# Token-major gates and branch projections, and regrouped up-projection matmuls, in a one-core decoder block

## The chip, the cores and the metric

The kernel runs on one core of a Trainium2 chip. A core has a matrix engine (TensorE, PE in the profile, with its weight loads listed apart as PEld), a vector engine (VectorE, DVE), a scalar engine (ScalarE, ACT), GpSimd (POOL) and a sync engine (SyncE, SP) that here issues the weight loads. They run side by side and meet by semaphores. On-chip memory is SBUF; TensorE writes its sums to PSUM, from which VectorE and ScalarE read. The metric is the device time of one execution in microseconds (us), the median of several runs.

## The reference, cut to what matters

One layer of a decoder trunk on 256 tokens of width 2048, all in float32. What is computed:

```python
mod = silu(c) @ w_ada + b_ada                      # 2048 x 12288, one row
h = rms_norm(x, g_pre_mix) * (1 + sc1) + sh1
p = h @ w_in + b_in                                # 2048 x 9216
u, v, q, k, v_att, z_pool, gates = split(p)        # six of 512 columns, gates 3 * 2048
y_sgu, y_moba, y_pool = ...                        # three branches, 512 wide each
g = sigmoid(gates)                                 # one per branch and channel
merged = g_sgu*(y_sgu@w_sgu_out) + g_moba*(y_moba@w_moba_out) + g_pool*(y_pool@w_pool_out)
x = x + gt1 * rms_norm(merged @ w_out, g_post_mix)
h = rms_norm(x, g_pre_ffn) * (1 + sc2) + sh2
z = conv3(h @ w_up) + b_conv                       # 2048 x 11264, causal, width 3 over tokens
gate, val = split(z)
x = x + gt2 * rms_norm((gelu(gate) * val) @ w_down, g_post_ffn)
```

## The kernel before

Every large product is made from three matmuls of rounded operands: an operand is split into a high part (fp32r) and a low part (what the rounding left), and high times high, high times low and low times high are added up in PSUM. Activations are split once. Each weight item, 4 chunks of 128 rows by 512 columns (1 MB), is loaded into one of 4 `raw` buffers, copied to `wh` by ScalarE and subtracted to `wl` by VectorE (`prep`, lines 291 to 320), so an item costs two ScalarE and two VectorE instructions of 128x1024. Six `wh` and six `wl` buffers hold three items.

Three routines do the matmuls of an item, all with 12,288 moving columns. `mm_b` (line 223) has weights stationary and the 256 tokens moving: channels come out on partitions, in 48 matmuls of 256 columns. `mm_a` (line 261) has 128 tokens stationary and 512 weight columns moving: tokens come out on partitions, in 24 matmuls of 512 columns. `mm_pairs` (line 241) has weights stationary and moves the high and the low activations, which lie side by side, as one 512-column matmul, followed by a 256-column one with the low weights: 16 such pairs. Its two sums lie in the two halves of a PSUM bank, and `join` (line 254) adds them, by a ScalarE copy and a VectorE add.

The twelve gate blocks (3 branches b by 4 column blocks j, named g00 to g23) are made in two ways. The six with j of 0 or 1 are in the input projection, which runs over k in four splits of 2, 4, 6 and 4 chunks, with `mm_b`, and the partial sums are added in SBUF (`block_use`, line 526). The six with j of 2 or 3 come later, whole, with `mm_pairs` (`gate_use`, line 504), as do the twelve branch projections (`branch_item`, line 783), whose joined result is multiplied by the gate and added up over b; after the third branch the sum is split into `mh` and `ml` for the output projection. Both need channels on partitions, as the output projection takes `mh` and `ml` as its stationary operand, and the bias of a gate is then one number for each partition, added by ScalarE with the sigmoid. PSUM has three buffers of two banks (`ps_acc`); an item of `mm_pairs` takes two of them, one of `mm_a` or `mm_b` takes one.

The order of work is a list of items: input projection, gates with j = 2, branches with j = 0, 1, 2, gates with j = 3, branches with j = 3, output projection, up and down projections of the feed-forward part. Between them are mixed the items of the conditioning product (`w_ada`), which VectorE accumulates (line 390). Each item's loads are issued 4 items ahead, its split is made up to 3 ahead; what follows its matmuls (`pending`) is issued ahead of the next item's matmuls, and the work on `side` one portion after each item. A scheduler then fixes the order on each engine; loads keep their order on SP's queue. The up projection (`up_item`, line 909) runs 88 items of `mm_pairs`: 24 for the first three column blocks in two halves of k, with the second half of `h2x` made between them (line 1112), and 64 in eight blocks with `mm_a` items of the down projection (tile `ps_dn`) in between.

Of the kernel before, what the change touches and what calls it, by code (L numbers as in the profile page):

```python
# [15 lines left out]
P = 128  # L16
# [10 lines left out]
P4_BUFS = 25  # L27
RAW_BUFS = 4
HL_BUFS = 6
JOIN_BUFS = 2  # L30
LOAD_AHEAD = 4
SPLIT_AHEAD = 3
SPLITS = (2, 4, 6, 4)
# [14 lines left out]
def kernel(  # L48
# [16 lines left out]
    joins = ctx.enter_context(tc.tile_pool(name="joins", bufs=JOIN_BUFS))  # L65
# [187 lines left out]

    def join(ps, dst=None):

        m = joins.tile([P, 2, 256], F32, name="join", tag="join") if dst is None else dst
# [244 lines left out]

    cur = {}

    def gate_use(name, kt0):

        def use(w):
            if kt0 == 0:
                cur[name] = [pair_ps("ps_" + name) for _ in range(2)]
            pss = cur[name]
            last = kt0 + 4 == KT  # L510
            mm_pairs(pss, w, hx_of(kt0), kt0 == 0, last)
            if not last:
                return

            def evac():
                g = gate[name] = p4(name)
                b, j = int(name[1]), int(name[2])
                for pr in range(2):
                    join(pss[pr], g[:, pr * 2:pr * 2 + 2])
                bias4(g, g, AF.Sigmoid, 24 + b * 16 + j * 4)  # L520
                if name == "g23":
                    load_sqrt(g[:, 3, 0:1])
            pending.append(evac)
        return use

    def block_use(name, kt0, nk, lo, hi):

        def use(hl_):
            if kt0 == lo:
                cur[name] = acc_ps("ps_" + name)  # L530
            ps = cur[name]
            last = kt0 + nk == hi
            (mm_a if name in "va" else mm_b)(ps, hl_, h_of(kt0), kt0 == lo, last)
            if not last:
                return

            def evac():
                final = hi == KT
                if lo == 0:
# [27 lines left out]
    def presplit_sigmoids(names):  # L567
        def f():
            for name in names:
                b, j = int(name[1]), int(name[2])  # L570
                bias4(gate[name], gate[name], AF.Sigmoid, 24 + b * 16 + j * 4)
        return f


# [207 lines left out]

    def branch_item(b, j):
        def use(w):
            pss = [pair_ps("ps_br") for _ in range(2)]
            mm_pairs(pss, w, lambda i: both(yx[b][i // 2], i % 2), True, True)

            def evac():
                g = gate[gate_name(b, j)]
                for pr in range(2):  # L790
                    gp = g[:, pr * 2:pr * 2 + 2]
                    nc.vector.tensor_tensor(gp, gp, join(pss[pr]), op=ALU.mult)
                if b:
                    g0 = gate[gate_name(0, j)]
                    nc.vector.tensor_tensor(g0, g0, g, op=ALU.add)
                    del gate[gate_name(b, j)]
                if b == 2:
                    mh[j], ml[j] = p4(f"mh{j}", dt=F32R), p4(f"ml{j}", dt=F32R)
                    split_act(mh[j], ml[j], g0)
                    del gate[gate_name(0, j)]  # L800
            pending.append(evac)
        w_item(w_branch[b], 0, 4, j * 512, use, pairs=True)


    ss2 = cp.tile([P, 2, 4], F32, name="ss2")
# [269 lines left out]

    def gate_full(j):
        for b in range(3):
            name = gate_name(b, j)
            for kt0 in range(0, KT, 4):
                w_item(w_in, kt0, 4, block_cols(name), gate_use(name, kt0), pairs=True)  # L1080

    def phase_mix():
        for j in rest[:-1]:
# [140 lines left out]
```

## Time and profile before

| | |
|---|---|
| time, median of 3 runs | 1438.35 us (1433.37 to 1439.8) |
| the profiled execution's own time | 1436.83 us |
| its span, first to last instruction | 1435.1 us |
| TensorE busy, weight loads | 1383.7 us, 1200.9 us |
| VectorE busy | 1120.9 us |
| ScalarE busy | 724.2 us |
| mean granted TensorE clock | 0.993 of full speed |

A busy TensorE is not one at its peak: matmuls are pipelined and the profile's duration of one (400 ns for 512 columns) is longer than the step from one to the next. Steps are read from a window: its length, divided by the matmuls in it.

### The profile page before, as it was taken

What the parts mean: (1) busy time and instruction counts of PE and PEld (TensorE: products, weight loads), DVE (VectorE), ACT (ScalarE), POOL (GpSimd) and SP (SyncE); (2) the same over time, 40 slices, a digit from 0 to 9 for tenths busy, and PEclk for the clock granted to TensorE, in tenths of its full rate; (3) what the DMA queues carried; (4) which work ended last, traced back from release to release, by engine and by line L of the source; (5) the groups of instructions that cost most, each with busy time, mean ns of one, the idle gap of its engine ahead of it and who ended that gap; (6) DMA issues with size and microseconds to landing.
All of it is one profiled execution on the core that took longest, in us unless ns stands there. A gap on an engine that the chain in (4) does not pass through costs nothing.

```text
span 1435.1 us, 20349 instructions
## 1 busy us (share of the span) xinstructions
PE 1383.7 (96%) x8095; PEld 1200.9 (84%) x8095; DVE 1120.9 (78%) x1463; ACT 724.2 (50%) x957; POOL 3.7 (0%) x12
## 2 busy tenths in 40 slices
PE   4998999999999999998999999999999999999997
PEld 3797999999888788886887888888888888888886
DVE  1289877689779988887988987879696867667676
ACT  4543534576855455345345654544444454545453
POOL 0000000000000000000000000000000000000000
PEclk9999999999999999999999999999999999999999
DMA  9799978855777798987985576676766765555551
GB/s 319 289 324 306 319 255 296 279 173 201 281 269 247 244 323 296 336 325 256 346 295 202 206 261 237 210 260 208 254 235 219 256 207 191 190 181 195 182 176 59
DMA packets 183022, 355.52 MB, mean 248 GB/s; under 512 B 5960, under 2 KB 20872, under 8 KB 182928
## 3 DMA queue, kind: packets, MB, share of 16 engines
q1 hardware_dynamic: 182076, 353.07, 71.0%
q8 instruction: 63, 1.03, 0.3%
q10 hardware_dynamic: 852, 1.16, 0.2%
q14 instruction: 31, 0.25, 0.0%
HBM read 352.11 MB, written 2.10 MB: 247 GB/s over the span
## 4 chain that ended last, share of the span: by engine, by line
PE 87%; DVE 7%; DMA 3%; ACT 1%; issue 1%; SPq 0%; DVEq 0%; ACTq 0%
PE ps_up L249 23%; PE ps_up L251 12%; PE ps_g L249 6%; PE ps_dn L273 6%; PE ps_dn L271 6%; PE ps_dn L272 6%; PE ps_g L251 3%; PE ps_g L234 3%; PE ps_g L232 3%; PE ps_g L233 3%; PE ps_out L273 2%; PE ps_out L272 2%; PE ps_out L271 2%; DMA raw<-in_w_in_dram 2%; DVE wl L302 2%; PE ps_br L249 1%
## 5 line engine op out<-in xcount | busy, mean ns | idle before, releaser
L249 PE MATMUL ps_up<-h2x,wh 128*128 128x512 f32 x1408 | 499.3, 400 | 5.3 <-DVE h2x L875 2.8
L301 ACT ACTIVATE wh<-raw 128x1024 fp32r<-128x1024 f32 x248 | 260.9, 1059 | 293.2 <-PE ps_up L249 135.6
L251 PE MATMUL ps_up<-h2x,wl 128*128 128x256 f32 x1408 | 395.9, 282 | 0.0
L302 DVE TENSOR_TENSOR wl<-raw,wh 128x1024 fp32r<-128x1024 f32 x248 | 301.3, 1222 | 106.9 <-ACT wh L301 105.6
L314 ACT ACTIVATE wh<-raw 128x1024 fp32r<-128x1024 f32 x228 | 227.5, 1012 | 253.8 <-PE ps_up L249 76.7
L315 DVE TENSOR_TENSOR wl<-raw,wh 128x1024 fp32r<-128x1024 f32 x228 | 261.7, 1167 | 96.7 <-ACT wh L314 96.1
L249 PEld LDWEIGHTS ps_up<-h2x,wh 128*128 128x128 f32 x1408 | 265.2, 189 | 71.0 <-issue 3.8
L251 PEld LDWEIGHTS ps_up<-h2x,wl 128*128 128x128 f32 x1408 | 267.3, 190 | 1.1 <-issue 0.5
L271 PE MATMUL ps_dn<-wh,ah 128*128 128x512 f32 x352 | 138.1, 392 | 0.0
L273 PE MATMUL ps_dn<-wh,al 128*128 128x512 f32 x352 | 137.2, 390 | 0.0
L272 PE MATMUL ps_dn<-wl,ah 128*128 128x512 f32 x352 | 137.2, 390 | 0.0
L249 PE MATMUL ps_g<-hx,wh 128*128 128x512 f32 x384 | 136.2, 399 | 0.0
L390 DVE SCALAR_TENSOR_TENSOR accb<-raw,cond,accb 128x512 f32<-128x512 f32 (+1 forms) x147 | 106.1, 722 | 10.7 <-DMA raw<-in_w_ada_dram 10.6
L390 DVE SCALAR_TENSOR_TENSOR acca<-raw,cond,acca 128x512 f32<-128x512 f32 (+1 forms) x155 | 112.2, 724 | 0.9 <-DMA acca<-in_b_ada_dram 0.8
L234 PE MATMUL ps_g<-hx,wl 128*128 128x256 f32 x384 | 109.2, 285 | 3.8 <-DVE wl L315 3.8
L232 PE MATMUL ps_g<-hx,wh 128*128 128x256 f32 x384 | 110.0, 286 | 2.3 <-ACT wh L314 2.3
L233 PE MATMUL ps_g<-hx,wh 128*128 128x256 f32 x384 | 108.8, 283 | 0.0
L251 PE MATMUL ps_g<-hx,wl 128*128 128x256 f32 x384 | 107.6, 281 | 0.0
L249 PEld LDWEIGHTS ps_g<-hx,wh 128*128 128x128 f32 x384 | 72.0, 188 | 17.3 <-issue 0.4
L271 PEld LDWEIGHTS ps_dn<-wh,ah 128*128 128x128 f32 x352 | 66.1, 188 | 14.2 <-issue 0.5
L272 PEld LDWEIGHTS ps_dn<-wl,ah 128*128 128x128 f32 x352 | 66.1, 188 | 13.9 <-issue 0.5
L234 PEld LDWEIGHTS ps_g<-hx,wl 128*128 128x128 f32 x384 | 73.7, 192 | 4.9 <-DVE wl L315 4.9
(246 smaller groups left out, 2015.4 us busy)
## 6 DMA issues: line engine op xcount, KB each, us to landing
raw<-in_w_up_dram SPq DMA_DIRECT2D x88, 1024.0 KB, 5.0
raw<-in_w_ada_dram SPq DMA_DIRECT2D x84, 1024.0 KB, 5.2
raw<-in_w_in_dram SPq DMA_DIRECT2D x54, 1024.0 KB, 6.1
raw<-in_w_down_dram SPq DMA_DIRECT2D x44, 1024.0 KB, 5.3
raw<-in_w_in_dram SPq DMA_DIRECT2D x24, 768.0 KB, 5.9
raw<-in_w_out_dram SPq DMA_DIRECT2D x16, 1024.0 KB, 7.0
raw<-in_w_ada_dram SPq DMA_DIRECT2D x16, 768.0 KB, 5.6
x<-in_x_dram SPq DMA_DIRECT2D x8, 512.0 KB, 7.2
```

What stands on the lines that cost most here:

```text
L232: nc.tensor.matmul(ps[:, nb], wh[:, s], xh, start=st, stop=False, skip_group_check=True)
L234: nc.tensor.matmul(ps[:, nb], wl[:, s], xh, start=False, stop=sp, skip_group_check=True)
L249: nc.tensor.matmul(ps[:, nb], wh[:, i, s], xhl, start=first and i == 0, stop=False, skip_group_check=True)
L251: nc.tensor.matmul(ps[:, nb, 256:512], wl[:, i, s], xh, start=False, stop=last and i == n - 1, skip_group_check=True)
L271: nc.tensor.matmul(psv[:, tt], xh[:, s], wh, start=st, stop=False)
L272: nc.tensor.matmul(psv[:, tt], xh[:, s], wl, start=False, stop=False)
L273: nc.tensor.matmul(psv[:, tt], xl[:, s], wh, start=False, stop=sp)
L301: nc.scalar.activation(h[:, :nk], it["raw"][:, :, cs], AF.Copy)
L302: nc.vector.tensor_tensor(l[:, :nk], it["raw"][:, :, cs], h[:, :nk].bitcast(F32), op=ALU.subtract)
L314: nc.scalar.activation(h[:, :n], it["raw"][:, k:k + n, cs], AF.Copy)
L315: nc.vector.tensor_tensor(l[:, :n], it["raw"][:, k:k + n, cs], h[:, :n].bitcast(F32), op=ALU.subtract)
L390: nc.vector.scalar_tensor_tensor(a, raw[:, kk], sc, a, op0=ALU.mult, op1=ALU.add)
```

## The change

The gates and the branch projections now go through `mm_a`, so their results have tokens on partitions. A gate's bias then runs along the row: it is loaded for all partitions from `b_in` (`gate_bias`, a 128x512 tile, 256 KB, on SP's queue), and VectorE adds it; ScalarE makes the sigmoid in one instruction. The branch result is multiplied by the gate straight from PSUM, without a join. After the third branch of a j the sum is transposed to channels on partitions by eight TensorE transposes (`merged_rows`, issued as side work), and split from PSUM. `mm_pairs`, now used by the up projection alone, issues the eight 512-column matmuls of a half item first, then its eight 256-column ones.

```diff
-                xh, xhl = act(i)
                 for nb in range(2):
-                    s = slice(nb * 128, nb * 128 + 128)
-                    nc.tensor.matmul(ps[:, nb], wh[:, i, s], xhl, start=first and i == 0, stop=False,
-                                     skip_group_check=True)
-                    nc.tensor.matmul(ps[:, nb, 256:512], wl[:, i, s], xh, start=False,
-                                     stop=last and i == n - 1, skip_group_check=True)
...
+                    nc.tensor.matmul(ps[:, nb], wh[:, i, nb * 128:nb * 128 + 128], act(i)[1],
+                                     start=first and i == 0, stop=False, skip_group_check=True)
+            for i in range(n):
+                for nb in range(2):
+                    nc.tensor.matmul(ps[:, nb, 256:512], wl[:, i, nb * 128:nb * 128 + 128], act(i)[0],
+                                     start=False, stop=last and i == n - 1, skip_group_check=True)
...
+    def gate_bias(name):
+
+        t = auxs.tile([P, 512], F32, name="gb", tag="aux")
+        ldma(t, bcast(b_in, block_cols(name), 512))
+        return t
...
-            (mm_a if name in "va" else mm_b)(ps, hl_, h_of(kt0), kt0 == lo, last)
+            if name[0] == "g" and last and hi == KT:
+                gb = gate_bias(name)[:, None, :].to_broadcast([P, 2, 512])
+            (mm_a if name[0] in "vag" else mm_b)(ps, hl_, h_of(kt0), kt0 == lo, last)
...
+                if (lo, hi) == (0, KT):
+                    g = gate[name] = p4(name)
+                    nc.vector.tensor_tensor(v2(g), v2(ps), gb, op=ALU.add)
+                    nc.scalar.activation(g, g, AF.Sigmoid)
...
-                    gate[name] = part[name]
+                    g = gate[name] = part[name]
+                    nc.vector.tensor_tensor(v2(g), v2(g), gb, op=ALU.add)
...
-                bias4(gate[name], gate[name], AF.Sigmoid, 24 + b * 16 + j * 4)
+                nc.scalar.activation(gate[name], gate[name], AF.Sigmoid)
...
-                for pr in range(2):
-                    gp = g[:, pr * 2:pr * 2 + 2]
-                    nc.vector.tensor_tensor(gp, gp, join(pss[pr]), op=ALU.mult)
+                nc.vector.tensor_tensor(g, g, ps, op=ALU.mult)
...
+                    side.append([lambda: merged_rows(j)])
...
+        for a in range(4):
+            for tt in range(2):
+                nc.tensor.transpose(pt[:, a, tt * 128:tt * 128 + 128], g[:, tt, a * 128:a * 128 + 128], ident)
+        mh[j], ml[j] = p4(f"mh{j}", dt=F32R), p4(f"ml{j}", dt=F32R)
+        split_act(mh[j], ml[j], pt)
```

`gate_use` is gone: `gate_full` calls `block_items` for whole gates. The two join buffers become two `aux` buffers, shared by the up projection's joins and the bias tiles.

TensorE in the up projection, before: `wh` and `wl` are the split weights, `h2x6` and `h2x7` the activations of two chunks of 128 rows each (high and low), `ps_up` the two PSUM buffers of an item.

```order
L249 MATMUL ps_up_8204<-h2x7_7049,wh_8247 128x512
L251 MATMUL ps_up_8204<-h2x7_7049,wl_8248 128x256
...
L249 MATMUL ps_up_8205<-h2x6_7048,wh_8251 128x512
L251 MATMUL ps_up_8205<-h2x6_7048,wl_8252 128x256
...
L249 MATMUL ps_up_8205<-h2x7_7049,wh_8251 128x512
```

The same place after:

```order
L247 MATMUL ps_up_6210<-h2x7_6095,wh_6156 128x512 x4
L251 MATMUL ps_up_6210<-h2x6_6094,wl_6157 128x256 x4
L251 MATMUL ps_up_6210<-h2x7_6095,wl_6157 128x256 x4
L247 MATMUL ps_up_6211<-h2x6_6094,wh_6160 128x512 x4
L247 MATMUL ps_up_6211<-h2x7_6095,wh_6160 128x512 x4
L251 MATMUL ps_up_6211<-h2x6_6094,wl_6161 128x256 x4
```

The two widths no longer alternate; the number of matmuls of each is what it was.

VectorE at the first branch projections, before: `ps_br` is the product in PSUM, `join` its joined halves, `part_g00` and `part_g10` gates, `acca` and `accb` the sums of the conditioning product.

```order
L258 TENSOR_TENSOR join_4313<-join_4313,ps_br_4269 128x512
L336 TENSOR_TENSOR sh2_128<-fin_4321,bada_116 128x4
L792 TENSOR_TENSOR part_g00_570<-part_g00_570,join_4313 128x512
L258 TENSOR_TENSOR join_4317<-join_4317,ps_br_4270 128x512
L302 TENSOR_TENSOR wl_4334<-raw_4303,wh_4333 128x1024
L792 TENSOR_TENSOR part_g00_570<-part_g00_570,join_4317 128x512
L302 TENSOR_TENSOR wl_4389<-raw_4371,wh_4388 128x1024
```

The same place after:

```order
L783 TENSOR_TENSOR part_g00_558<-part_g00_558,ps_br_3582 128x1024
L336 TENSOR_TENSOR sh2_128<-fin_3618,bada_116 128x4
L315 TENSOR_TENSOR wl_3631<-raw_3607,wh_3630 128x1024
L390 SCALAR_TENSOR_TENSOR acca_3573<-raw_3624,cond_109,acca_3573 128x512
L390 SCALAR_TENSOR_TENSOR accb_3574<-raw_3624,cond_109,accb_3574 128x512
L390 SCALAR_TENSOR_TENSOR acca_3573<-raw_3624,cond_109,acca_3573 128x512
L315 TENSOR_TENSOR wl_3670<-raw_3659,wh_3669 128x1024
L783 TENSOR_TENSOR part_g10_604<-part_g10_604,ps_br_3634 128x1024
L315 TENSOR_TENSOR wl_3674<-raw_3659,wh_3673 128x1024
L786 TENSOR_TENSOR part_g00_558<-part_g00_558,part_g10_604 128x1024
```

Two joins and two multiplications of 128x512 for each branch item became one multiplication of 128x1024.

SP's queue ahead of the last gates of the input projection, before: `raw` are the weight buffers.

```order
L288 DMA raw_3197<-in_w_in_dram 128x4x512
L288 DMA raw_3277<-in_w_in_dram 128x4x512
L288 DMA raw_3363<-in_w_ada_dram 128x4x512
L288 DMA raw_3433<-in_w_in_dram 128x4x512
L288 DMA raw_3517<-in_w_in_dram 128x4x512
L288 DMA raw_3575<-in_w_ada_dram 128x4x512
```

The same place after: `gb` is a bias tile, of which there are two buffers.

```order
L82 DMA gb_2672<-in_b_in_dram 128x512
L288 DMA raw_2722<-in_w_in_dram 128x4x512
L288 DMA raw_2781<-in_w_in_dram 128x4x512
L82 DMA gb_2735<-in_b_in_dram 128x512
L288 DMA raw_2846<-in_w_ada_dram 128x4x512
L82 DMA gb_2794<-in_b_in_dram 128x512
L288 DMA raw_2895<-in_w_in_dram 128x4x512
```

The weight loads behind a `gb` now stand behind its wait for a buffer.

## Rows read from the trace of the kernel before

**Rows 1.** Page, part 1: engine, busy us, share of the span, instructions.

```profile
PE 1383.7 (96%) x8095; PEld 1200.9 (84%) x8095; DVE 1120.9 (78%) x1463; ACT 724.2 (50%) x957; POOL 3.7 (0%) x12
```

**Rows 2.** Page, part 4: the chain that ended last, by engine.

```profile
PE 87%; DVE 7%; DMA 3%; ACT 1%; issue 1%; SPq 0%; DVEq 0%; ACTq 0%
```

**Rows 3.** Windows: us, busy PE, PEld, DVE, ACT, POOL (instructions), granted clock, DMA.

```profile
60.00:150.00 90.00, 82.36 (x624) 75.89 (x623) 76.50 (x112) 40.96 (x47) 0.00 (x0) 1.00 0.95 322
150.00:300.00 150.00, 150.00 (x1146) 145.24 (x1146) 116.89 (x139) 75.25 (x95) 2.84 (x5) 1.00 0.81 275
421.12:482.63 61.51, 55.96 (x306) 48.31 (x305) 60.25 (x82) 31.86 (x42) 0.00 (x0) 0.94 0.69 233
430.00:490.00 60.00, 54.45 (x294) 46.86 (x293) 60.00 (x81) 29.30 (x36) 0.00 (x0) 0.94 0.70 242
```

**Rows 4.** Waits from 421 to 483 us: waiter, releaser, us, times, longest.

```profile
PEld ps_br L249 <- DVE join L258: 6.6, 4, 3.1
ACT join L257 <- DVE part_g L792: 6.5, 3, 4.9
PE ps_br L249 <- DVE join L258: 5.6, 3, 2.7
```

**Rows 5.** TensorE in order of time: start, us, line, tiles, idle before.

```profile
455.20 0.80 PE L249 MATMUL ps_br<-yx,wh 128*128 128x512 f32 x1 [2.40 <-DVE join L258]
```

**Rows 6.** TensorE in a window, tile ps_g by mm_b: 256 columns each.

```profile
216.76:255.63 38.87, 38.87 (x324) 1.00 0.86 300
```

**Rows 7.** The same, tile ps_dn by mm_a: 512 columns each.

```profile
1113.34:1135.15 21.81, 21.81 (x96) 1.00 0.69 234
```

**Rows 8.** The same, tile ps_up by mm_pairs: 512 and 256 columns in turn.

```profile
1135.16:1180.36 45.20, 45.20 (x256) 1.00 0.68 235
1000.68:1045.45 44.77, 44.77 (x256) 1.00 0.69 236
672.13:689.00 16.87, 16.87 (x96) 1.00 0.73 249
```

**Rows 9.** The same, tile ps_g by mm_pairs, gates with j = 2 and 3.

```profile
398.41:421.11 22.70, 22.70 (x128) 1.00 0.84 293
506.05:539.41 33.36, 33.36 (x192) 1.00 0.91 324
```

**Rows 10.** The same, tile ps_br by mm_pairs, branches with j = 3.

```profile
551.38:568.07 16.69, 16.69 (x96) 1.00 0.84 276
```

**Rows 11.** VectorE in order of time, branch stage.

```profile
441.39 1.29 DVE L792 TENSOR_TENSOR part_g<-part_g,join 128x512 f32<-128x512 f32 x2
442.59 1.22 DVE L302 TENSOR_TENSOR wl<-raw,wh 128x1024 fp32r<-128x1024 f32 x1
443.73 1.22 DVE L795 TENSOR_TENSOR part_g<-part_g,part_g 128x1024 f32<-128x1024 f32 x1
```

**Rows 12.** TensorE in order of time: eight transposes.

```profile
382.15 1.04 PE L757 MATMUL at_pt<-ident,s 128*128 128x128 f32 x8
382.94 0.48 PE L249 MATMUL ps_g<-hx,wh 128*128 128x512 f32 x1
```

**Rows 13.** TensorE in order of time, between the halves of the first up blocks.

```profile
744.20 0.95 PE L326 MATMUL fin<-ones,acca 128*128 128x1 f32 x8
745.01 2.03 PE L215 MATMUL ptx<-d,x 128*128 128x128 f32 x16
749.15 0.50 PE L249 MATMUL ps_up<-h2x,wh 128*128 128x512 f32 x1 [2.10 <-DVE h2f L874]
```

**Rows 14.** Groups of weight loads: busy us, mean ns, idle before.

```profile
L251 PEld LDWEIGHTS ps_up<-h2x,wl 128*128 128x128 f32 x1408 | 267.3, 190 | 1.1 <-issue 0.5
```

**Rows 15.** Groups of VectorE: addition of a bias row to 128x1024.

```profile
L490 DVE TENSOR_TENSOR part_a<-part_a,bvb 128x1024 f32<-128x1024 f32 x1 | 1.2, 1220 | 0.0
```

**Rows 16.** DMA issues of two tiles: KB each, median us to landing.

```profile
raw<-in_w_in_dram SPq DMA_DIRECT2D x54, 1024.0 KB, 6.1
bvb<-in_b_in_dram SPq DMA_DIRECT2D x2, 256.0 KB, 7.0
```

More of the change, by code (lines that the diff above doesn't have):

```diff
@@ L29 @@
 HL_BUFS = 6
-JOIN_BUFS = 2
+AUX_BUFS = 2
 LOAD_AHEAD = 4
@@ L64 @@
     accs = ctx.enter_context(tc.tile_pool(name="accs", bufs=4))
-    joins = ctx.enter_context(tc.tile_pool(name="joins", bufs=JOIN_BUFS))
+    auxs = ctx.enter_context(tc.tile_pool(name="auxs", bufs=AUX_BUFS))
     ps_acc = ctx.enter_context(tc.tile_pool(name="ps_acc", bufs=3, space=bass.MemoryType.PSUM))
@@ L245, in mm_pairs, with join @@
             for i in range(n):
-                xh, xhl = act(i)
                 for nb in range(2):
-                    s = slice(nb * 128, nb * 128 + 128)
-                    nc.tensor.matmul(ps[:, nb], wh[:, i, s], xhl, start=first and i == 0, stop=False,
-                                     skip_group_check=True)
-                    nc.tensor.matmul(ps[:, nb, 256:512], wl[:, i, s], xh, start=False,
-                                     stop=last and i == n - 1, skip_group_check=True)
-    def join(ps, dst=None):
-        m = joins.tile([P, 2, 256], F32, name="join", tag="join") if dst is None else dst
+                    nc.tensor.matmul(ps[:, nb], wh[:, i, nb * 128:nb * 128 + 128], act(i)[1],
[4 more added lines that the diff above has]
+                                     start=False, stop=last and i == n - 1, skip_group_check=True)
+    def join(ps):
+        m = auxs.tile([P, 2, 256], F32, name="join", tag="aux")
         nc.scalar.activation(m, ps[:, :, 256:], AF.Copy)
@@ L502 @@
     cur = {}
[L504 to L517, printed above, removed]
-                for pr in range(2):
[L519 to L524, printed above, removed]
+    def gate_bias(name):
+        t = auxs.tile([P, 512], F32, name="gb", tag="aux")
+        ldma(t, bcast(b_in, block_cols(name), 512))
+        return t
     def block_use(name, kt0, nk, lo, hi):
@@ L538, in evac @@
                 final = hi == KT
+                if (lo, hi) == (0, KT):
+                    g = gate[name] = p4(name)
+                    nc.vector.tensor_tensor(v2(g), v2(ps), gb, op=ALU.add)
+                    nc.scalar.activation(g, g, AF.Sigmoid)
+                    if name == "g23":
+                        load_sqrt(g[:, 3, 0:1])
+                    return
                 if lo == 0:
@@ L784, in use @@
         def use(w):
-            pss = [pair_ps("ps_br") for _ in range(2)]
-            mm_pairs(pss, w, lambda i: both(yx[b][i // 2], i % 2), True, True)
+            ps = acc_ps("ps_br")
+            mm_a(ps, w, lambda i: (yx[b][i // 2][:, i % 2, 0], yx[b][i // 2][:, i % 2, 1]), True, True)
             def evac():
                 g = gate[gate_name(b, j)]
-                for pr in range(2):
-                    gp = g[:, pr * 2:pr * 2 + 2]
-                    nc.vector.tensor_tensor(gp, gp, join(pss[pr]), op=ALU.mult)
+                nc.vector.tensor_tensor(g, g, ps, op=ALU.mult)
                 if b:
@@ L797, in evac, with merged_rows @@
                 if b == 2:
-                    mh[j], ml[j] = p4(f"mh{j}", dt=F32R), p4(f"ml{j}", dt=F32R)
-                    split_act(mh[j], ml[j], g0)
-                    del gate[gate_name(0, j)]
+                    side.append([lambda: merged_rows(j)])
             pending.append(evac)
-        w_item(w_branch[b], 0, 4, j * 512, use, pairs=True)
+        w_item(w_branch[b], 0, 4, j * 512, use)
+    def merged_rows(j):
+        g = v2(gate.pop(gate_name(0, j)))
+        pt = acc_ps("pt_m")
+        for a in range(4):
[3 more added lines that the diff above has]
+        split_act(mh[j], ml[j], pt)
     ss2 = cp.tile([P, 2, 4], F32, name="ss2")
@@ L1077, in gate_full @@
         for b in range(3):
-            name = gate_name(b, j)
-            for kt0 in range(0, KT, 4):
-                w_item(w_in, kt0, 4, block_cols(name), gate_use(name, kt0), pairs=True)
+            block_items([gate_name(b, j)], 0, KT)
     def phase_mix():
```

1 line of the change is left out of this document (removed).

## The prediction

> **What bounds the kernel now.** I read the page's busy times first: TensorE is busy for 1383.7 of 1435.1 us [rows 1], and the chain that ended last is TensorE for 87% and VectorE for 7% [rows 2]. So the question is what a matmul costs, and where TensorE stands still. The windows answer the second. From 150 to 300 us TensorE has no gap; from 60 to 150 it lacks 7.6 us, with the DMA engines busy for 0.95; in the nine branch items from 421.1 to 482.6 it lacks 5.6 us and the mean granted clock falls to 0.94, while VectorE works 60.00 of the 60 us from 430 to 490 [rows 3]. The waits name what is late there: TensorE and its weight loads wait for `join` on VectorE, that is for a PSUM buffer, and ScalarE's `join` waits for VectorE's multiplication to free a join buffer [rows 4]. One such wait is 2.40 us long, and the 512-column matmul behind it takes 0.80 us [rows 5].
>
> The first question I answer by steps, a window's length over its matmuls. With 256 columns throughout (`mm_b`) it is 38.87 / 324 = 120.0 ns [rows 6], with 512 throughout (`mm_a`) 21.81 / 96 = 227.2 ns [rows 7]. Two of 256 cost 12.8 ns more than one of 512: beside its columns every matmul costs some 13 ns. A 512 and a 256 in turn should cost 347.2 ns. In the up projection a pair costs 45.20 / 128 = 353.1 ns in seven of the eight blocks; one has 349.8, and the first items 351.5 [rows 8]. The gates have 354.7 for j = 2 and 347.5 for j = 3 [rows 9], the last branches 347.7 [rows 10]. So alternating costs between nothing and 7.5 ns a pair above the sum of its parts.
>
> **The change part by part.** The sum is made against the profiled execution, 1436.83 us (its span and 1.7 us around it), which lies 1.5 us under the median of 1438.35.
>
> Gates of the input projection. A chunk of k costs 12 x 120.0 = 1440 ns as `mm_b` and 6 x 227.2 = 1363 ns as `mm_a`, 77 ns less. Six gates have the chunks 6 to 16 in stretches where TensorE never waits: 60 x 77 ns = 4.6 us. Chunks 0 to 6 lie in or ahead of the stretch that waits for weights: of their 2.8 us I count the 0.9 that comes behind its last wait; bounds 0 and 2.8. Together -5.5. The bias costs VectorE six additions of about 1.2 us [rows 15]. They fall in stretches where the splits run items ahead of their use (no wait of TensorE from 150 to 300), so I take nothing; uncovered they would cost 7.
>
> Gates with j = 2 and 3, 24 items. An item becomes 24 x 227.2 = 5.453 us, from 16 x 354.7 = 5.675 and 16 x 347.5 = 5.560: 12 x 0.222 + 12 x 0.107 = 4.0 us less. VectorE has one addition of 128x1024 for two of 128x512, ScalarE one sigmoid for two copies and four.
>
> The nine branch items from 421.1 on. They took 61.51 us. What remains for TensorE is 9 x 5.453 = 49.1, two groups of eight `fin` at 0.81 [rows 13], and three groups of eight transposes at 0.79 [rows 12]: 53.1 us, so at most 8.4 less. VectorE steps 0.60 us for each join and multiplication and 1.14 for 128x1024 [rows 11]; an item loses 4 x 0.60 and gains 1.14, nine of them 11.3 us less. It was saturated beyond the stage, so its work there comes to 49 to 56 us, about TensorE's own. A PSUM buffer no longer limits: an item takes one of three, not two. What is late next is the transpose. It stands one item (5.45 us) behind the third product, and ahead of it VectorE must do a multiplication, an addition and up to two `wl` in between, 4 x 1.14 = 4.6 us: a lag over 0.9 us stops TensorE, with the following item behind it. I take 2.5 us for the three, between 0 and 8.4, nearer to 0 since VectorE loses more work than the gap was long. Net -5.9. The last three branch items go from 16.69 to 16.36 us, but eight transposes come on top: +0.5.
>
> For the transposes, eight step from 382.15 to 382.94 at a granted clock of 1.00 on either side, so 32 cost 3.2 us, all counted above. [...]
>
> The up projection, 88 items. Eight 512 and eight 256 in a row should step as rows 6 and 7 do, 347.2 ns for one of each. Seven blocks of 128 pairs gain 5.9 ns each: 5.3 us. Of the 24 earlier items, the second dozen gains 192 x 4.3 ns = 0.8 us; the first dozen gains nothing, since behind it TensorE waits anyway for the second half of h2, the wait that ends at 749.15 [rows 13]. Together -6.1. Bounds: 0, if the excess is not from alternating, and 8.3, if all 1408 pairs gain 5.9. The `wl` are needed later than before, which can only help.
>
> Twelve bias tiles of 256 KB on SP's queue. The nearest row landed in 7.0 us, a weight item in 6.1 [rows 16]. A `gb` waits until the one two gates earlier has been added, and the loads behind it wait too, but they are for items four or more ahead (22 us). I take 0; uncovered, one landing for each of the six whole gates, 42 us, is the far bound, and VectorE would stand in the queue ahead of the splits.
>
> Sum: -5.5 - 4.0 - 5.9 + 0.5 - 6.1 = -21.0 us. From 1436.83 that is 1415.8 for a profiled execution, 1417 for the median.
>
> **The rivals.**
> *Only the regrouping brings nothing.* The excess of alternating pairs varies between stretches of the same code (353.1 and 349.8), so it may come from something that regrouping leaves. Then -14.9: 1423.
> *TensorE's time goes by columns alone.* All three routines move 12,288 columns an item; if the steps do not carry over, only the branch wait goes. With 16 x 347.5 ns for an item the stage has 61.51 - 50.0 - 1.6 - 2.4 - 2.5 = 5.0 us to give, less 0.8 for the last transposes: 1434. The steps of 120.0 and 227.2 speak against it, that both come from other stretches speaks for it. The Trainium skill, the same page, section "Back-to-back issue gap", adds only 2.5 ns to N / 2.4 for each matmul; by that, 24 matmuls for 32 save 20 ns an item, not the 107 to 222 above, and the time would be near this rival's. Here the step of 227.2 lies 13.9 ns above 512 / 2.4, so the trace does not agree.
> *All early gains and all waits count.* Chunks 0 to 6 in full (+1.9), no wait at the transposes (+2.5), every up pair (+2.2): 1410.
> *Slower: eight weight loads in a row show.* A weight load is listed at 190 ns [rows 14]; in pairs, every second one hides behind a 512-column matmul. If the eight 256-column matmuls of the up projection wait for their loads, seven of eight step at 190 and not 120: 1408 x 7/8 x 70 ns = 86 us against the 14.9 that the rest brings: 1438 + 71 = 1509. It decides from a step of about 136 ns on, where the regrouping eats the rest. Against it stands `mm_b`, where matmuls of 256 columns with a listed load each run at 120.0.
> *The loads behind a waiting `gb` come late.* It would show as waits of ScalarE's splits for `raw`, and turn part of the gain into TensorE gaps: within 1426 to 1436.
>
> **How the numbers follow.** Forecast 0.56, regrouping without gain 0.14, columns alone 0.10, all gains 0.09, late loads 0.07, slower 0.04. The forecast's own range is 1411 to 1424. The whole range, 1407 to 1430, takes in the first, second and fourth case and part of the fifth. About 0.5% (7.2 us) is what a measurement can tell from no change: faster by more is below 1431.2. That holds for the forecast, the second and the fourth case and half of the late loads: 0.83. Columns alone and the other half are within 0.5%: 0.12. Slower: 0.05.
>
> **What would show it.** In the profile after: windows of `ps_g` and `ps_br` with 227 ns a matmul; half items of `ps_up` with 2.78 us; in the branch stage no wait of TensorE for a PSUM buffer, at most short ones ahead of `pt_m`, a granted clock of 1.00 throughout and a stage of 53 to 56 us; the wait for h2 still there, a little longer. The prediction is wrong if the 256-column rows step well over 120 ns, if VectorE waits for `gb`, or if TensorE stands at `pt_m` for more than some 3 us each time.

## The result, and the profile after

The changed kernel takes 1417.1 us (median of 4 runs, 1413.29 to 1420.13), the one before on the same chip 1436.6: a ratio of 0.9863 with an interval of [0.9828, 0.9897]. A second comparison on another chip (below) gave 0.9874 [0.9849, 0.9900]. The execution that was profiled took 1416.88 us with a span of 1415.2, to be set against 1436.83: 19.95 us less.

The page's busy times and the chain that ended last, as in [rows 1, 2]:

```profile
PE 1370.6 (97%) x7263; PEld 1161.0 (82%) x7263; DVE 1112.6 (79%) x1427; ACT 699.3 (49%) x885; POOL 5.1 (0%) x12
PE 90%; DVE 4%; DMA 3%; ACT 2%; issue 1%; SPq 0%; DVEq 0%; ACTq 0%
```

VectorE's share of the chain has fallen from 7 to 4%. The windows that answer to [rows 3]; the branch stage now begins at 414.21 and ends at 467.04 us (columns as there):

```profile
60.00:150.00 90.00, 82.54 (x465) 68.67 (x464) 79.34 (x114) 42.91 (x49) 0.00 (x0) 0.97 0.96 331
150.00:300.00 150.00, 150.00 (x895) 134.23 (x894) 116.95 (x139) 74.14 (x94) 4.25 (x5) 1.00 0.81 273
414.21:467.04 52.83, 52.71 (x249) 44.06 (x248) 50.35 (x57) 21.79 (x21) 0.00 (x0) 1.00 0.82 285
```

The branch stage is 52.83 us for 61.51, TensorE lacks 0.1 us in it, and the granted clock is 1.00 from end to end. From 60 to 150 us, where the loads bind, nothing has come in: TensorE lacks as much as before.

Windows of TensorE with one tile alone (length, busy, matmuls, clock, DMA): the gates in the input projection, j = 2, j = 3, the last branches, an ordinary up block, the one block that had been short, and three of the first up items, as in [rows 6, 8 to 10]:

```profile
216.05:252.80 36.75, 36.75 (x162) 1.00 0.89 310
392.32:414.21 21.89, 21.89 (x96) 1.00 0.86 309
490.50:523.30 32.80, 32.80 (x144) 1.00 0.92 327
535.05:551.37 16.32, 16.32 (x72) 1.00 0.81 275
849.07:893.73 44.66, 44.66 (x256) 1.00 0.69 245
983.30:1028.38 45.08, 45.08 (x256) 1.00 0.69 240
675.32:692.17 16.85, 16.85 (x96) 1.00 0.99 347
```

Divided by the matmuls, the gates step at 226.9 to 228.0 ns and the branches at 226.7: `mm_a`'s step of [rows 7] has moved to its new places. The up blocks went from 45.20 to 44.66 us, the short one from 44.77 to 45.08, and the first items from 16.87 to 16.85.

TensorE in order of time around a group of transposes of the merged result, and further on between the first and the second dozen of up items (start, duration, line, tiles, idle before), the place of [rows 13]:

```profile
454.14 0.95 PE L326 MATMUL fin<-ones,acca 128*128 128x1 f32 x8
455.21 1.06 PE L799 MATMUL pt_m<-ident,part_g 128*128 128x128 f32 x8
456.03 0.48 PE L271 MATMUL ps_br<-wh,yx 128*128 128x512 f32 x1
...
729.87 0.48 PE L247 MATMUL ps_up<-h2x,wh 128*128 128x512 f32 x1
730.19 1.11 PE L251 MATMUL ps_up<-h2x,wl 128*128 128x256 f32 x8
731.14 0.95 PE L326 MATMUL fin<-ones,acca 128*128 128x1 f32 x8
734.89 1.65 PE L247 MATMUL ps_up<-h2x,wh 128*128 128x512 f32 x3 [2.80 <-DVE h2f L873]
```

Eight transposes take 0.82 us from start to next matmul, and what stands ahead of them is short: `fin` steps 1.07 us here for some 0.81 elsewhere. The wait for h2 is still there, 2.80 us for 2.10. The bias tiles `gb`, their use and what waited (engine, operation, durations; then what VectorE sat idle for ahead of the additions, and the landing of the DMAs):

```profile
L82 SPq DMA_DIRECT2D gb<-in_b_in_dram x12: 341/497/1007, 291.9 to 520.9; - x12
L527 DVE TENSOR_TENSOR g<-ps_g,gb x6: 1216/1222/1225, 370.0 to 535.2; 128x1024 f32<-128x1024 f32 x6
...
  PE ps_g L273: 0.8, 2
...
DMA to landing us min/median/max: 5.2/5.8/6.1
```

VectorE waited for TensorE before these additions, 0.8 us in two places, and never for a `gb`.

Where the 19.95 us are, from the starts of the same TensorE work in both traces (negative is gained):

| stretch | before, us | after, us | difference | predicted |
|---|---|---|---|---|
| start to branch stage (input projection, gates j = 2) | 421.12 | 414.21 | -6.9 | -8.2 |
| nine branch items | 61.51 | 52.83 | -8.7 | -6.7 (1) |
| gates j = 3 (after: with 0.8 of transposes) | 68.75 | 68.01 | -0.7 | -0.5 |
| last branch items | 16.69 | 16.32 | -0.4 | -0.3 |
| to the first up item (0.9 of transposes) | 104.06 | 105.81 | +1.8 | +0.8 |
| first dozen up, to the end of the wait | 77.02 | 77.71 | +0.7 | 0 |
| second dozen up | 72.62 | 70.64 | -2.0 | -0.8 |
| up and down blocks to the last matmul of `ps_up` | 560.52 | 556.82 | -3.7 | -5.3 |
| rest | 52.8 | 52.8 | 0 | 0 |

(1) The predicted -5.9 held three groups of transposes; one of them lies in the gates of j = 3, 0.8 us.

### The profile page after: what moved, and what is told of

Its sections match the earlier page's. It is cut to its first block, busy times and chain, and to the rows that moved or that the text cites. A ratio compares the mean times of both kernels' runs of the same rounds, so it can differ in the third digit from the quotient of the medians.

```text
span 1415.2 us, 18580 instructions
## 1 busy us (share of the span) xinstructions
PE 1370.6 (97%) x7263; PEld 1161.0 (82%) x7263; DVE 1112.6 (79%) x1427; ACT 699.3 (49%) x885; POOL 5.1 (0%) x12
## 4 chain that ended last, share of the span: by engine, by line
PE 90%; DVE 4%; DMA 3%; ACT 2%; issue 1%; SPq 0%; DVEq 0%; ACTq 0%
PE ps_up L247 23%; PE ps_up L251 12%; PE ps_dn L271 6%; PE ps_dn L272 6%; PE ps_dn L273 6%; PE ps_g L272 6%; PE ps_g L271 6%; PE ps_g L273 6%; PE ps_out L273 2%; PE ps_out L271 2%; PE ps_out L272 2%; PE ps_br L271 2%; PE ps_br L272 2%; PE ps_br L273 2%; DMA raw<-in_w_ada_dram 1%; DMA raw<-in_w_in_dram 1%
## 5 line engine op out<-in xcount | busy, mean ns | idle before, releaser
L314 ACT ACTIVATE wh<-raw 128x1024 fp32r<-128x1024 f32 (+1 forms) x300 | 303.9, 1024 | 373.3 <-PE ps_g L273 92.3
L315 DVE TENSOR_TENSOR wl<-raw,wh 128x1024 fp32r<-128x1024 f32 (+1 forms) x300 | 348.5, 1179 | 109.6 <-ACT wh L314 108.8
L247 PE MATMUL ps_up<-h2x,wh 128*128 128x512 f32 x1408 | 356.6, 395 | 4.2 <-DVE h2f L873 2.8
L301 ACT ACTIVATE wh<-raw 128x1024 fp32r<-128x1024 f32 x176 | 185.6, 1060 | 214.3 <-PE ps_up L247 127.9
L302 DVE TENSOR_TENSOR wl<-raw,wh 128x1024 fp32r<-128x1024 f32 x176 | 214.3, 1222 | 84.2 <-ACT wh L301 83.8
L251 PEld LDWEIGHTS ps_up<-h2x,wl 128*128 128x128 f32 x1408 | 192.0, 190 | 13.8
L251 PE MATMUL ps_up<-h2x,wl 128*128 128x256 f32 x1408 | 196.3, 282 | 0.0
L271 PE MATMUL ps_g<-wh,hx 128*128 128x512 f32 x384 | 152.7, 398 | 2.9 <-ACT wh L314 2.9
L272 PE MATMUL ps_g<-wl,hx 128*128 128x512 f32 x384 | 151.6, 395 | 3.8 <-DVE wl L315 3.8
L273 PE MATMUL ps_g<-wh,hx 128*128 128x512 f32 x384 | 150.6, 392 | 0.0
L271 PEld LDWEIGHTS ps_g<-wh,hx 128*128 128x128 f32 x384 | 72.7, 189 | 20.7 <-ACT wh L314 4.7
L273 PEld LDWEIGHTS ps_g<-wh,hx 128*128 128x128 f32 x384 | 72.7, 189 | 15.1
```

Of the source, the lines that this page charges most:

```text
L247: nc.tensor.matmul(ps[:, nb], wh[:, i, nb * 128:nb * 128 + 128], act(i)[1], start=first and i == 0, stop=False, skip_group_check=True)
L251: nc.tensor.matmul(ps[:, nb, 256:512], wl[:, i, nb * 128:nb * 128 + 128], act(i)[0], start=False, stop=last and i == n - 1, skip_group_che ...
L271: nc.tensor.matmul(psv[:, tt], xh[:, s], wh, start=st, stop=False)
L272: nc.tensor.matmul(psv[:, tt], xh[:, s], wl, start=False, stop=False)
L273: nc.tensor.matmul(psv[:, tt], xl[:, s], wh, start=False, stop=sp)
L301: nc.scalar.activation(h[:, :nk], it["raw"][:, :, cs], AF.Copy)
```

## The experiments

The eleven runs ask four things: what ends the branch stage, what sets a matmul's step in the gates, what the rows of eight are worth in the up projection, and what the wait ahead of the second dozen is. All are edits of the changed kernel, but for two: one edits the kernel before, one is the changed kernel as it stands.

**1. The rows of eight undone.**

```diff
             for i in range(n):
+                xh, xhl = act(i)
                 for nb in range(2):
-                    nc.tensor.matmul(ps[:, nb], wh[...], act(i)[1], ...)
-            for i in range(n):
-                for nb in range(2):
-                    nc.tensor.matmul(ps[:, nb, 256:512], wl[...], act(i)[0], ...)
+                    s = slice(nb * 128, nb * 128 + 128)
+                    nc.tensor.matmul(ps[:, nb], wh[:, i, s], xhl, ...)
+                    nc.tensor.matmul(ps[:, nb, 256:512], wl[:, i, s], xh, ...)
```

> The changed kernel with one part undone: mm_pairs alternates 512 and 256 columns again, and only the up projection uses it. Theory (alternating costs some ns a pair above its parts): an up block of 128 pairs takes 45.2 us again instead of 44.67, the second dozen of up items loses some 2 us, the first dozen nothing; together 4 to 6 us longer than the changed kernel, so about 1422 us where that has 1417. Rival (the up blocks got shorter because of what lies around them: bias tiles, fewer buffers waited for): blocks stay at 44.7 us and the time at 1417. The branch stage stays at 53 us in both.

It takes 1423.1 us (4 runs), ratio 0.9884 [0.9861, 0.9907] to the kernel before. That interval overlaps the changed kernel's, so the totals do not settle it; the traces do. The up part, from the first to the last matmul of `ps_up`, is 708.7 us for 705.2: the rows of eight are worth 3.55 us between these two executions, not 6.1. Most of the rest, 2.3 us, lies ahead of the branch stage, where the code is the same. The same windows of `ps_up`: an ordinary block, the short one without its first 0.4 us, three of the first items:

```profile
851.69:896.90 45.21, 45.21 (x256) 1.00 0.69 235
987.45:1031.82 44.37, 44.37 (x256) 1.00 0.69 234
677.68:694.41 16.73, 16.73 (x96) 1.00 1.00 353
```

The same code steps at 353.2 ns a pair in one block, at about 347 in another, and at 348.5 in the first items (their start included). The first dozen is 76.3 us here and 77.7 with rows; the second 71.9 and 70.6. So the rows lose 1.4 us at first, win that back in the second dozen and gain 3.65 in the blocks. The gain in the blocks repeats: from the end of the second dozen to the last matmul of `ps_up` it is 556.8 us in all nine profiled executions with rows of eight, and 560.5 in both with alternation. What the dozens win and lose is mostly waits for h2: at the end of the first 2.80 us for 2.11, inside the second 1.4 for 2.8. TensorE's busy time is no shorter with rows there (second dozen, changed kernel, then experiment 1):

```profile
734.89:805.53 70.64, 69.26 (x385) 0.98 0.60 209
736.23:808.16 71.93, 69.04 (x385) 0.98 0.61 206
```

Nor do the dozens repeat well: in experiment 3, with the same code there, the second takes 73.9 us, at a mean granted clock of 0.94. For the blocks, the steps from one matmul's start to the next show where the gain is (ns, worked out from the starts in the trace; numbers over 200 are those of 512 columns):

```
alternating, ordinary block:  113 233 117 241 120 236 | 113 233 117 241 120 236 | ...   353.3 a pair
alternating, short block:     117 230 116 230 117 230 | 117 230 116 230 117 230 | ...   346.6 a pair
alternating, first items:     118 231 112 232 118 230 | 113 232 118 231 112 232 | ...   347.0 a pair
rows of eight, any block:     233 236 228 233 230 227 227 227  113 120 120 120 120 120 120 120   349.0 a pair
```

An alternating stream runs in one of two rhythms and keeps it through each of the eight blocks. The faster is the sum of the parts, 227.2 + 120.0; the slower, in which seven of the eight blocks ran, is 6 ns a pair above it. The fast one is the third block in both traces with alternation, the only one whose first matmul stands right behind the two of `gtrow`. The rows of eight have one rhythm, with some 20 ns lost on the 512s after a 256 and 6 won back on the first 256.

**2. Only the rows, in the kernel before.** The kernel before, with the same regrouping for all that `mm_pairs` did there, the gates and branches too (the edit of experiment 1 the other way round).

> The kernel before with one part alone: mm_pairs issues eight 512-column and then eight 256-column matmuls, for the gates, the branches and the up projection. Theory (the branch stage waits for PSUM buffers that VectorE frees late, and width order has no part in it): up blocks at 44.67 us, gates with j = 2 at 349 ns a pair, but the branch stage still 58 to 62 us with waits of TensorE for join; in all 5 to 7 us shorter than before, about 1431. Rival (the branch stage waited for the low weights, which grouped rows need later): the stage falls to 55 us or less, and the time to about 1424.

1433.3 us (10 runs) for 1439.3, ratio 0.9958 [0.9941, 0.9976]: by the totals regrouping alone is worth some 6 us of the 20, with 3.5 to 8.5 in the interval. The execution that was profiled (1436.0, one of the slowest of the ten) has the blocks' 3.7 us in full and gives 1.4 of it back in the dozens. The gates of j = 2 and 3, then the branch stage with all engines:

```profile
400.44:422.90 22.46, 22.46 (x128) 1.00 0.88 300
507.17:540.78 33.61, 33.61 (x192) 1.00 0.91 325
...
422.90:484.01 61.11, 54.54 (x306) 47.53 (x305) 60.22 (x81) 32.14 (x43) 0.00 (x0) 0.97 0.70 234
```

In rows the gates step at 350.9 and 350.1 ns a pair, 5.60 to 5.61 us an item for the 5.47 of `mm_a`; against [rows 9] j = 2 gains and j = 3 loses, two rhythms again. The branch stage, in rows too, stays at 61 us: VectorE is busy for 60.22 of it. The order of the widths was not its bound.

**3. VectorE loaded again.** Two additions of 128x512 more on VectorE for each branch item; their sums are not used.

```diff
+                for pr in range(2):
+                    t = auxs.tile([P, 2, 256], F32, name="dum", tag="aux")
+                    nc.vector.tensor_tensor(t, g[:, pr * 2:pr * 2 + 2], g[:, pr * 2:pr * 2 + 2], op=ALU.add)
```

> The changed kernel with two extra VectorE additions of 128x512 behind each branch multiplication, 1.2 us an item, which gives VectorE its work of before back while an item still takes one PSUM buffer. Their results are not used. Theory V (VectorE's work was the bound of the stage): the nine branch items take 57 us or more instead of 52.8, with TensorE waiting ahead of the transposes. Theory P (the PSUM and join buffers were the bound; VectorE can run late with one buffer an item): the stage stays within 1.5 us of 52.8, and VectorE's backlog is worked off in the gates behind it.

1430.4 us. The branch stage with all engines, and TensorE's longest wait in it (waiter, releaser, us, times, longest):

```profile
416.93:478.09 61.16, 54.26 (x250) 45.21 (x249) 58.91 (x72) 22.01 (x21) 0.00 (x0) 0.97 0.73 248
...
PE pt_m L802 <- DVE part_g L789: 6.9, 2, 4.5
```

The stage is back at the length of before, with PSUM, transposes and matmuls as in the changed kernel. Sixteen of the eighteen additions fall into the stage, at 0.60 us each [rows 11], and one `wl` less: VectorE is busy for 58.91 us in place of 50.35, 8.6 more, and the stage is 8.3 longer. VectorE's work sets the stage, and the wait shows at the transposes, the place that the prediction named.

**4. Two PSUM buffers for a branch item again.** The matmuls stay 512 columns wide; each token half has its own buffer, and VectorE multiplies each by itself.

```diff
-            ps = acc_ps("ps_br")
-            mm_a(ps, w, ..., True, True)
+            pss = [acc_ps("ps_br") for _ in range(2)]
+            ...
-                nc.vector.tensor_tensor(g, g, ps, op=ALU.mult)
+                for tt in range(2):
+                    nc.vector.tensor_tensor(g[:, tt * 2:tt * 2 + 2], ..., pss[tt][:, :2], op=ALU.mult)
```

> The changed kernel with each branch item's two token halves in two PSUM buffers of three, as before, and two multiplications of 128x512 (1.2 us) in place of one of 128x1024 (1.14 us). Theory V (VectorE's work was the bound): the stage stays at 53 to 54 us. Theory P (the number of buffers was the bound): TensorE waits for PSUM again, each item's first matmul for the multiplication of the item ahead, and the stage takes 57 us or more, with the granted clock below 1.00 in it.

1415.6 us. The branch stage, and TensorE's wait for a PSUM buffer in it:

```profile
410.22:464.49 54.27, 53.25 (x250) 43.89 (x248) 51.65 (x65) 22.00 (x21) 0.00 (x0) 1.00 0.82 284
...
PE ps_br L784 <- DVE g L791: 0.7, 1, 0.7
```

54.27 us, 1.4 more, beside 1.3 us more of VectorE's work, and one wait of 0.7 us for a buffer. The freed buffer was not what shortened the stage; taken with experiment 3, the 5.6 us wait for `join` of [rows 4] was VectorE being late, seen through a buffer. (The shorter total lies ahead of 410 us, see below.)

**5. The gates in 256 columns.** Tokens stay on partitions; each 512-column matmul of a gate becomes two of 256.

```diff
-            (mm_a if name[0] in "vag" else mm_b)(ps, hl_, h_of(kt0), kt0 == lo, last)
+            (mm_an if name[0] == "g" else mm_a if name in "va" else mm_b)(ps, hl_, h_of(kt0), kt0 == lo, last)
```

> The changed kernel with each of the gates' matmuls cut into two of 256 columns (tokens stay on the partitions, the sums are the same): 48 matmuls of 256 columns an item for 24 of 512. If every matmul costs some 13 ns beside its columns, whichever operand is stationary, the step is 120.0 ns and an item 5.76 us for 5.45: 24 whole gates cost 7.4 us more and the input projection's gates up to 60 x 77 ns = 4.6 us, together 1426 to 1430 in the profiled execution. If instead the orientation sets the step (weights streaming, activations stationary), the step is 113.6 ns, the item stays at 5.45 us and the time at 1417.

1430.3 us. The gates of the input projection and of j = 3:

```profile
216.82:255.70 38.88, 38.88 (x324) 1.00 0.90 308
501.21:535.84 34.63, 34.63 (x288) 1.00 0.86 305
```

120.0 and 120.2 ns a matmul: the orientation is worth nothing by itself. What the change gains in the gates is that 24 matmuls pay the 13 ns beside the columns, and not 32 or 48.

**6. Rows of sixteen, and of four.** Sixteen: both halves' 512s, then both halves' 256s. Four: two chunks at a time.

```diff
         for ps, (wh, wl, n) in zip(pss, w):
             for i in range(n):
                 for nb in range(2):
                     nc.tensor.matmul(ps[:, nb], ...)          # 512 columns
+        for ps, (wh, wl, n) in zip(pss, w):
             for i in range(n):
                 for nb in range(2):
                     nc.tensor.matmul(ps[:, nb, 256:512], ...) # 256 columns
```

> The changed kernel with rows twice as long in the up projection: sixteen 512-column matmuls, then sixteen of 256. The steps after the change show some 21 ns lost on the first six 512s after a 256 and 6 ns won back on the first 256. If each change of width costs about 14 ns net, half as many changes give 348.1 ns a pair and 44.56 us a block for 44.67, and the up part is about 1.2 us shorter: some 1416. If the 349.0 ns a pair have another cause, the block stays at 44.67.

> The changed kernel with rows half as long in the up projection: four 512-column matmuls, then four of 256. If each change of width costs about 14 ns net, twice as many changes give 350.8 ns a pair and 44.90 us a block for 44.67, and the up part is about 2.5 us longer. If the 349.0 ns a pair have another cause, the block stays at 44.67; if only strict alternation is dear, too.

Sixteen: 1418.7 us (4 runs), ratio 0.9872 [0.9841, 0.9904], not told apart from the changed kernel. Four: 1421.5. A block with sixteen (the last), then one with four:

```profile
1319.60:1364.23 44.63, 44.63 (x256) 1.00 0.60 199
...
851.88:896.76 44.88, 44.88 (x256) 1.00 0.70 240
```

Four costs 0.22 us a block, as the price of a change of width would have it (44.90 expected). With sixteen most items take 5.567 us for 5.587, 20 ns less, but the block gains only 0.03: its fifth item, in which the built order puts four of the 256s ahead of the second eight 512s, takes 5.68 to 5.79. The trace lists no wait there; why it costs 0.1 to 0.2 us stays open.

**7. Half of VectorE's conditioning work left out.** The first dozen up items are mixed with multiplications of the conditioning (`acca`, `accb`).

```diff
+                    if half and k >= 8:
+                        continue
```

> The changed kernel without the upper half (chunks 8 to 15) of VectorE's multiplications for the conditioning items that are mixed into the first dozen up items; their sums are then left incomplete. If the first dozen ends with a wait for the second half of h2 because VectorE is late with it, the wait of 2.8 us ahead of the second dozen shrinks below 1 us and the dozen takes 75 us or less for 77.7. If the wait for h2 has another cause (TensorE's own sums, ScalarE), dozen and wait stay as they are, 77.7 and 2.8 us.

It takes 1415.6 us. TensorE between the dozens, and VectorE just before:

```profile
728.59 0.95 PE L326 MATMUL fin<-ones,acca 128*128 128x1 f32 x8
731.86 3.54 PE L247 MATMUL ps_up<-h2x,wh 128*128 128x512 f32 x8 [2.32 <-DVE h2f L875]
...
724.77 0.69 DVE L932 TENSOR_TENSOR upart<-upart,ps_up 128x512 f32<-128x512 f32 x1 [6.62 <-ACT upart L929]
```

The theory missed: the dozen takes 77.2 us and the wait is still there, 2.32 us, although VectorE now sits idle for 6.6 us just before. In the changed kernel's trace h2's input is transposed from 719.34 on and its scale is ready at 711.5, but ScalarE's first eviction of h2 stands in its order behind a copy of an up result, which TensorE delivers at 726.7; ScalarE is idle for 7.69 us ahead of that copy, here as there (changed kernel):

```profile
719.34 1.95 PE L215 MATMUL ptx<-d,x 128*128 128x128 f32 x16
...
726.69 0.60 ACT L927 ACTIVATE upart<-ps_up 128x512 f32<-128x512 f32 x1 [7.69 <-PE ps_up L251]
727.19 0.56 ACT L872 ACTIVATE h2x<-ptx,sh,s 128x256 fp32r<-128x256 f32 x1
```

**8. h2 made earlier**, beside the changed kernel unedited on the same chip. A quarter of h2 (chunks 8 to 11) is made three up items earlier.

```diff
+        if i == 0:
             call(lambda lo=lo, hi=hi: h2_part(lo, hi))
+        else:
+            ups = [x for x, it in enumerate(items) if it["kind"] == "w"]
+            items.insert(ups[-3], dict(kind="call", use=lambda: h2_part(8, 12)))
+            call(lambda: h2_part(12, 16))
```

> The changed kernel with chunks 8 to 11 of h2 made three up items earlier (the second half of the conversion stays where it is). Theory Q (order of the queues): the 2.8 us wait ahead of the second dozen comes from ScalarE's and VectorE's order, in which h2's eviction stands behind the copy of the last up result, a copy that waits for TensorE, although its input and scale have been there some 6 us longer; then the wait goes, TensorE's first 512-column row runs through, and the run is 2 to 3 us shorter than the changed kernel's: about 1414. Rival: the second half of h2, whose shift comes from a sum that ends with the dozen, sets the end; then a wait of like length stands one item (5.6 us) later and the time stays at 1417.

> The changed kernel itself, unedited, beside the one with the earlier h2 on the same chip: 1417, ratio 0.986 to the kernel before. Under theory Q it is 2 to 3 us above the other, under the rival equal to it.

1415.7 us (1412.94 to 1416.99) for 1419.25 (1417.64 to 1420.98), ratios 0.9852 [0.9823, 0.9882] and 0.9874. The total looks as theory Q had it; the trace does not. TensorE between the dozens, and VectorE in the same stretch:

```profile
728.51 0.95 PE L326 MATMUL fin<-ones,acca 128*128 128x1 f32 x8
732.24 3.47 PE L247 MATMUL ps_up<-h2x,wh 128*128 128x512 f32 x8 [2.77 <-DVE upart L930]
...
725.59 0.76 DVE L390 SCALAR_TENSOR_TENSOR acca<-raw,cond,acca 128x512 f32<-128x512 f32 x1
...
727.39 0.70 DVE L393 TENSOR_TENSOR acca<-acca,accb 128x512 f32<-128x512 f32 x1
727.99 3.51 DVE L302 TENSOR_TENSOR wl<-raw,wh 128x1024 fp32r<-128x1024 f32 x3
731.39 1.30 DVE L930 TENSOR_TENSOR upart<-upart,ps_up 128x512 f32<-128x512 f32 x2
```

The wait has changed its cause and kept its length. Now TensorE wants a PSUM buffer, whose eviction stands on VectorE behind an addition and three `wl`, made late by eight multiplications ahead of them (the last is shown). The whole up part is 703.9 us for 705.2; of the other 4.7 us between the two profiles 4.5 lie ahead of the branch stage, where the instructions are the same. Each of the two was profiled once, so what share of the medians' 3.5 us is chance in that stretch is not shown. Both the theory and its rival were wrong on the wait.

**9. Both at once**, the edits of 7 and 8.

> The early h2 and, at once, without the upper half (chunks 8 to 15) of VectorE's multiplications for the conditioning items in the first dozen up items, whose sums are left incomplete. Each edit alone left a wait of 2.8 to 3.3 us ahead of the second dozen. Theory T (two causes behind one another, ScalarE's order of h2 behind an up copy and VectorE's backlog ahead of the PSUM eviction): without both the wait falls below 1 us and the first dozen takes 75 us or less for 77.7. Rival (a third cause at this place, such as TensorE's sums for the conditioning between the dozens): the wait stays at 2 us or more.

TensorE between the dozens, and its window of the second dozen:

```profile
731.06 0.95 PE L326 MATMUL fin<-ones,acca 128*128 128x1 f32 x8
731.87 2.09 PE L247 MATMUL ps_up<-h2x,wh 128*128 128x512 f32 x8
...
731.87:800.15 68.28, 67.59 (x386) 1.00 0.64 218
```

1411.5 us, and no wait there (the next, one item later, is 0.7 us): the first dozen takes 74.7 us, the up part 699.8. Two causes stood behind one another, and each alone left the wait at 2.3 to 2.8 us. More goes with the wait than its own length: the granted clock, at half from 734.6 to 738.0 us in the changed kernel, from the end of the wait on, stays at 1.00 here, and the second dozen takes 68.3 us for 70.6, with a wait of 0.7 us in it for 1.4.

## Why the prediction came out right, step by step

*What bounds the kernel.* Held: steps of TensorE, and in the branch stage VectorE. Experiments 2 to 4 show the second from three sides.

*Gates.* The sizes held: 5.47 us for an item of j = 2 (5.45 predicted), 36.75 us where [rows 6] had 38.87. That the gain is one of the count of matmuls, not of what is stationary, is experiment 5. The 0.9 us counted for the early chunks cannot be found. They lie where the loads bind, and that stretch varies by itself: the ten executions whose instructions stand in one order up to the branch stage (the changed kernel twice, experiments 1, 3, 4, both of 6, 7, 8 and 9) reach it at 414.2, 416.1, 416.5, 416.9, 410.2, 415.2, 414.7, 411.7, 411.7 and 414.8 us. In the window from 118 to 165 us the granted clocks differ too (changed kernel, experiment 4, experiment 1):

```profile
118.00:165.00 47.00, 40.76 (x170) 31.97 (x169) 42.30 (x59) 21.42 (x27) 2.55 (x4) 0.93 0.94 326
...
118.00:165.00 47.00, 41.94 (x197) 33.97 (x196) 45.02 (x62) 21.02 (x28) 2.55 (x4) 0.96 0.95 329
...
118.00:165.00 47.00, 43.01 (x174) 34.53 (x173) 41.51 (x59) 20.90 (x26) 0.45 (x2) 0.85 0.94 325
```

Of these three, the earlier the stage is reached (414.2, 410.2 and 416.5 us), the higher the clock; over the ten that does not hold, as experiments 8 and 3 (411.7 and 416.9 us) both have 0.93. Whether late loads lower the clock or both have one cause wasn't tried. So -6.9 for a predicted -8.2 is within what this stretch does by itself.

*The branch stage.* The mechanism held, the size was off: -8.7 where the table has -6.7. The term that was mis-sized is the 2.5 us for waits at the transposes: with 52.3 us as TensorE's own work (nine items, two `fin`, two groups of transposes) the stage of 52.83 leaves 0.5. VectorE's 50.35 lies just under it, and experiment 3 shows how little spare there is.

*Transposes.* Four groups cost 0.79 to 0.87 us each, 99 to 109 ns a transpose, and the granted clock is 1.00 around all four. The Trainium skill, "TensorE: Matmul & The Clock Gate", Part 4 on PE-mode transpose, has some 275 ns in a kernel: the trace agrees with it as one transpose's listed duration (270 to 299 ns), not as its step.

*Between branches and up projection.* +0.9 us beyond the transposes wasn't foreseen. The granted clock is at half, 1.2 GHz, from 649 to 656 us there, and 1.00 throughout that stretch before; of the other runs it falls there in all but experiments 2 and 3. Ahead of the fall TensorE was busy for 7.11 of 9.20 us, and in the same 9 us of the kernel before, which kept its clock, for 7.07 of 9.00. The 0.9 us go with the fall: experiment 3, with the same code there and no fall, takes 104.66 us, 0.6 over the kernel before and no more than its transposes, and experiment 9, where the clock is at half from 650.8 to 654.2 us only, takes 105.25. Why the clock falls stays open.

*The up projection.* Sum of -5.0 for a predicted -6.1. The term of the blocks was mis-sized: they step at 349.0 and not 347.2 ns a pair, 0.23 us a block. That is the change of width, which the sum had put at nothing (experiment 6). The dozens came to -1.3 for a predicted -0.8, and not by the steps that the prediction counted: TensorE's busy time in them fell by 0.5 us, and the rest is waits for h2, 2.80 us for 2.10 at the end of the first and 1.4 for 2.8 inside the second. Why the second is shorter was not tried; this part is luck. That the first dozen gains nothing was right, as the wait behind it stayed; what makes that wait is the order on ScalarE and, behind it, VectorE's backlog (experiments 7 to 9).

*Bias tiles.* Nothing, as taken; they landed in 5.8 us and nobody waited for one.

*The rivals.* Slower by weight loads: the 256s in rows step at 120 ns, experiment 1's list. Columns alone: refuted by experiment 5. The formula of the Trainium skill that the prediction sets beside this rival ("TensorE: Matmul & The Clock Gate", section "Back-to-back issue gap") is given there for an isolated matmul, not for a stream with a weight load ahead of each, so it was not that page's rule for this kernel. Regrouping without gain: it gains 3.55 us, a bit more than half. All gains: of its three terms only the waits at the transposes came in. Late loads behind a `gb`: from 285 to 560 us ScalarE's splits wait 9.0 us for `raw`, 7.6 before, and TensorE has no wait that the trace lists. In the prediction's last sums, columns alone and half of the late loads are 0.135 by its own list, where it has 0.12, and slower is 0.04, where it has 0.05. By the table the terms missed by +4.6 us where they promised too much and by -3.5 where too little: the total of 1417 owes its closeness to that.

## What to carry to other kernels

Count matmuls as well as columns: with a weight load each they cost some 13 ns beside their columns here, so fewer and wider is a gain whichever operand is stationary. A wait for a PSUM buffer may be a wait for the engine that empties it, which two looks tell apart: that engine's share of the stage, and a run with its work raised. Before a wait is priced, see what stands queued behind what on the engine that releases it, and what would release it next: one cause taken away alone can leave the wait as long as it was.

## What the runs showed of the hardware that was not expected

- An alternating stream of 512 and 256 columns has two stable rhythms, 347.0 and 353.3 ns a pair, in the same code; it keeps one through each of the up projection's blocks. What picks it was not tried.
- A change from 256 to 512 columns and back costs some 12 to 16 ns net in rows of sixteen, four and eight: about 20 lost on the first five 512s (233, 236, 228, 233, 230 for 227) and 6 won back on the first 256.
- Ten executions of the same first instructions differ by up to 6.7 us where the branch stage begins, more than the rows of eight are worth. The total credits experiment 8 with 3.5 us, where its edit gained 1.3 in the up projection.
- The wait behind the first dozen ends at half the granted clock (734.6 to 738.0 us); with the wait gone (experiment 9) that fall is gone too.
